# Differential attention on one core: the product with V moved behind the scores and into the turn's PSUM banks, fill split by kind of turn

## The chip, the core and the metric

The kernel runs on one core of one Trainium2 chip. The core has five engines that run side by side, each through its own list of instructions in order: TensorE (PE; its weight loads are shown apart as PEld), VectorE (DVE), ScalarE (ACT), GpSimd (POOL) and SyncE (SP, which here only issues transfers). They wait for each other by semaphores. The metric is the device time of one execution in microseconds (us); less is better.

## What is computed

One layer of an encoder with two branches, on a sequence of 1024 tokens of width 1024, in float32. The part that the change touches is the attention branch; the other branch (a state-space scan) and the projections around both are as before.

```
q = partial_rope(q); k = partial_rope(k)          # 4 heads, 2 halves of 64 each
def block(qblk):                                  # 128 queries
    sc = jnp.einsum('bqhcd,bkhcd->bhcqk', qblk, k) * scale
    p = jax.nn.softmax(sc, axis=-1)
    w = p[:, :, 0] - lam * p[:, :, 1]
    return jnp.einsum('bhqk,bkhe->bqhe', w, v)
o = rmsnorm(o, g_subln) * (1.0 - lam_init)
attn_branch = (o.reshape(b, s, ATTN_WIDTH) * jax.nn.silu(z_a)) @ w_up_attn
merged = jax.nn.sigmoid(g_a) * attn_branch + jax.nn.sigmoid(g_s) * ssm_branch
return x + gate[:, None, :] * (merged @ w_out)
```

Float32 products are made of three matmuls each, on operands that are cut into a high and a low part (`split`: ACT copies the high part, DVE or POOL subtracts it and leaves the low part).

## The kernel before

The program has five stretches: input norm and the first projections, the state-space branch, its gate and up-projection, the attention (stage 3, some 464 to 762 us of the trace), and the last two projections. The change lies in stage 3 and in the few us behind it.

**Turns.** Stage 3 goes through 32 turns g = 0 to 31, eight per head (head g // 8, and i = g % 8 within it), each for 128 queries, and two more (32, 33) that finish. PE's list for a turn, before the change: `qk(g)`, the scores, eight matmuls of 512 columns (`sc`, lines 1423 and 1424) into two tiles of two banks; fill; in every odd turn from 3 on `pv`, the product of two finished turns with V, 24 matmuls of 256 columns (`pv`, line 1465); `transpose_w(g-1)`, eight transposes of the weights `e` of the turn before (`tp<-cst,e`, line 1454); fill again. Meanwhile DVE takes the maximum of the scores (`nm`, line 1425, two reductions of 1024), ACT the exponentials (`e<-sc`, two), and DVE the mix of the two softmax halves of the turn before (`mix(g-1)`: `zr`, `wm`, and `e<-e,wm` of 1024 columns). The transposes of turn g wait for this mix. Behind them ACT copies the high part (`wth`, two of 512) and DVE makes the low part (`wtl`, two), which `pv` reads in one of the next two turns.

**Fill.** Between these stands work that needs nothing of the turn: the projections of q, k and v of the next head (heads 0 to 2) and gates (head 3). `drive` takes units of fill off the generator `s3_fill` whenever `s3_main` yields an amount: FA = 3.1 behind the scores and FB = 1.0 behind the transposes (2.45 and 1.0 from turn 24 on). One unit is three matmuls of 512 columns (`mm<-hh,wh`, `hl,wh`, `hh,wl`, line 217); a *block* below is one such unit. Eight blocks make half a projection, whose result ACT evicts (`rq`, `vt` or `side`). Small follow-up steps hang on the fill (`with_pend`, `rope_unit`): the rotation of q and k of the next head takes a shuffle on DVE into the tile `rs` (tag "tb", one buffer), three operations on POOL (times sine, times cosine, sum), and later ACT's copy `rh` and POOL's low part. The weights of the next projection are cut by ACT (`wh`) and POOL (`wl`).

**Per head.** `spot(s, g)` puts three things of a head into fixed turns of the next head, by the table `EV`: `make_v` (eight transposes of v, evicted by ACT `vh` and DVE `vl`) at the end of turn i = 1, `o_turn` (eight transposes of the finished output, evicted by ACT) at the end of i = 2, `o_norm` from the end of i = 3 on (eight short squares on ACT, `jk`; the rest in one go on DVE in i = 4; the scaling `o<-o,nry` on POOL), and `o_back` (eight transposes back, evicted by DVE `of`) at the end of i = 5, behind which SP stores the result.

**PSUM.** Eight banks: four for scores (tag "sc"), two of `ps_mm` (tag "mm") and two of `ps3` (tag "tp"). The pair "mm" is used by fill in turn with `pv`; the pair "tp" by the transposes of weights, V and output. A tile takes the older bank of its pair and waits until that was evicted. The order of every engine is the order in which the program records its instructions; no scheduler changes it.

Of the kernel before, what the change touches and what calls it, by code (L numbers as in the profile page):

```python
# [18 lines left out]
P = 128  # L19
# [47 lines left out]
def tile_hybrid_block(  # L67
# [1389 lines left out]
    def pv(p):  # L1457
# [3 lines left out]
        ps = ps_mm.tile([P, 512], F32, tag="mm", name="pv")  # L1461
# [19 lines left out]
    def o_norm(h, e=G, big=None):  # L1481
        H = heads[h]
        on, zr = H["on"], H["zr"]
        ss = po.tile([P, 8], F32, tag="oss", name="oss")
        if big is None:
            for t in range(8):
                jk = po.tile([P, P], F32, tag="jk", name="jk")
                act(jk, on[:, t], AF.Square, scale=zr[:, t, 0:1], accum_out=ss[:, t:t + 1])
            yield
        else:  # L1490
            z2 = po.tile([P, 8], F32, tag="jk", name="z2")
            for hf in range(2):
                act(big[:, hf * 512:hf * 512 + 512], H["o"][:, hf * 512:hf * 512 + 512], AF.Square)
            yield
            mul(z2, zr[:, :, 0], zr[:, :, 0])
            V.tensor_reduce(out=ss, in_=big[:].rearrange("p (t e) -> p t e", t=8), axis=AX.X, op=ALU.add)
            mul(ss, ss, z2)
        res = []
        for _ in rsqrt_gen(po, ss, 8, 1.0 / P, "o", res):
            yield  # L1500
        rs = res[0]
        mul(rs, rs, zr[:, :, 0])
        yield
        mul(on, on, bc(rs[:], 2, [P, 8, P]), e)
# [15 lines left out]
    def s3_main():  # L1520
# [6 lines left out]
        def spot(s, g):  # L1527
# [3 lines left out]
            if (i, s) == EV["v"] and h < 4:  # L1531
                make_v(h)
            if (i, s) == EV["turn"]:
                o_turn(h - 1)
            if (i, s) == EV["za"]:
                load_za(h - 1)
            if (i, s) == EV["sq"]:
                gens[h] = o_norm(h - 1)
                next(gens[h])
            if (i, s) == EV["norm"]:  # L1540
                run_all(gens[h])
            if (i, s) == EV["back"]:
                of = o_back(h - 1)
                SP.dma_start(out=ofd[h - 1], in_=of)

        for g in range(NG + 2):
            fa, fb = (FA, FB) if g < 24 else (LA, LB)
            if g < NG:
                qk(g)
            if 1 <= g <= NG:  # L1550
                mix(g - 1)
            spot(0, g)
            yield fa
            spot(1, g)
            if g >= 3 and g % 2 == 1:
                pv((g - 3) // 2)
            if 1 <= g <= NG:
                transpose_w(g - 1)
            spot(2, g)
            yield fb / 2  # L1560
            spot(3, g)
            yield fb / 2
# [225 lines left out]
```

## Time and profile before

| | before |
|---|---|
| median of 3 runs | 928.51 us (928.42 to 929.39) |
| the profiled execution: its time, its span | 930.2 us, 928.3 us |
| mean granted TensorE clock | 0.986 |
| busy: PE, PEld, DVE, ACT, POOL | 95%, 79%, 71%, 40%, 18% of the span |
| instructions | 12225 |
| last chain: PE, DVE, ACT, issue | 68%, 19%, 5%, 3% of the span |

The page and the answers give times from the start of the span. A row of the view of waits says which engine (and line) waited for whom, how long in total, how often, and the longest. A row of the timeline gives the start, the time from the first start to the last end, engine, line, operation, out<-in, sizes, how many were merged, and in brackets the idle time of the engine before it and what ended it. Matmuls overlap: one that takes 0.39 us is followed by the next 0.23 us later. A row of the view by lines ends with busy time, mean duration in ns, and the idle time before the group. A row of the view by windows gives the stretch, its length, busy time of the five engines, and the granted clock.

### The profile page before, as it was taken

What the parts mean: (1) busy time and instruction counts of PE and PEld (TensorE: products, weight loads), DVE (VectorE), ACT (ScalarE), POOL (GpSimd) and SP (SyncE); (2) the same over time, 40 slices, a digit from 0 to 9 for tenths busy, and PEclk for the clock granted to TensorE, in tenths of its full rate; (3) what the DMA queues carried; (4) which work ended last, traced back from release to release, by engine and by line L of the source; (5) the groups of instructions that cost most, each with busy time, mean ns of one, the idle gap of its engine ahead of it and who ended that gap; (6) DMA issues with size and microseconds to landing.
All of it is one profiled execution on the core that took longest, in us unless ns stands there. A gap on an engine that the chain in (4) does not pass through costs nothing.

```text
span 928.3 us, 12225 instructions
## 1 busy us (share of the span) xinstructions
PE 882.2 (95%) x4528; PEld 731.3 (79%) x4528; DVE 662.2 (71%) x1234; ACT 375.4 (40%) x652; POOL 164.9 (18%) x128
## 2 busy tenths in 40 slices
PE   5999999999999998999999999998998999999996
PEld 4878878888888886787778877787777788888885
DVE  5987999998999964673667576755866655573465
ACT  6753532322222253301365456545645544232222
POOL 1001000000000004222234425435411111340000
PEclk9899899999999999999999999999999999999998
DMA  9926223243433554593433313313123123958022
GB/s 297 301 74 182 87 74 116 82 125 96 129 99 91 168 167 175 185 351 122 113 81 91 80 34 103 97 51 85 61 71 89 49 89 116 339 183 304 13 88 95
DMA packets 106478, 119.57 MB, mean 129 GB/s; under 512 B 7587, under 2 KB 87696, under 8 KB 106418
## 3 DMA queue, kind: packets, MB, share of 16 engines
q1 hardware_dynamic: 104628, 114.08, 40.0%
q10 hardware_dynamic: 1614, 4.51, 1.2%
q8 instruction: 36, 0.59, 0.3%
q0 software_dynamic: 176, 0.20, 0.1%
q14 instruction: 24, 0.20, 0.1%
HBM read 78.46 MB, written 27.73 MB: 114 GB/s over the span
## 4 chain that ended last, share of the span: by engine, by line
PE 68%; DVE 19%; ACT 5%; issue 3%; DMA 2%; POOL 1%; SPq 1%; ACTq 0%; DVEq 0%
PE mm L217 38%; PE op L1707 10%; PE pv L1465 5%; DVE nm L1425 3%; PE tp L1454 3%; PE sc L1423 2%; PE sc L1424 2%; ACT e L99 2%; DVE acc L96 2%; DVE cb L78 2%; PE yp L1050 1%; DVE wl L78 1%; PE w L1002 1%; DVE e L96 1%; DVE wtl L78 1%
## 5 line engine op out<-in xcount | busy, mean ns | idle before, releaser
L217 PE MATMUL mm<-hh,wh 128*128 128x512 f32 x592 | 238.1, 402 | 0.5 <-ACT o L99 0.5
L217 PE MATMUL mm<-hh,wl 128*128 128x512 f32 x592 | 232.0, 392 | 0.0
L217 PE MATMUL mm<-hl,wh 128*128 128x512 f32 x592 | 231.8, 392 | 0.0
L217 PEld LDWEIGHTS mm<-hh,wl 128*128 128x128 f32 x592 | 111.7, 189 | 24.1 <-DVE wl L78 0.5
L217 PEld LDWEIGHTS mm<-hh,wh 128*128 128x128 f32 x592 | 111.9, 189 | 23.5 <-issue 1.6
L217 PEld LDWEIGHTS mm<-hl,wh 128*128 128x128 f32 x592 | 112.0, 189 | 20.9
L99 ACT ACTIVATE e<-sc,nm 128x1024 f32<-128x1024 f32 x64 | 71.1, 1114 | 71.8 <-DVE nm L1425 71.8
L78 DVE TENSOR_TENSOR wtl<-tp,wth 128x512 fp32r<-128x512 f32 x64 | 41.2, 686 | 70.7 <-ACT wth L99 70.7
L1425 DVE TENSOR_REDUCE nm<-sc 128x1 f32<-128x1024 f32 x64 | 75.4, 1219 | 22.4 <-PE sc L1424 21.6
L78 POOL TENSOR_TENSOR wl<-wr,wh 128x1024 fp32r<-128x1024 f32 x22 | 53.5, 2430 | 185.9 <-ACT wh L99 185.8
L99 ACT ACTIVATE wh<-wr 128x1024 fp32r<-128x1024 f32 x49 | 51.7, 1057 | 64.4 <-DMA pad<-pt 21.2
L99 ACT ACTIVATE side<-mm 128x512 f32<-128x512 f32 x48 | 28.6, 597 | 107.2 <-PE mm L217 78.9
L1423 PE MATMUL sc<-kk,qq 128*128 128x512 f32 x128 | 50.6, 395 | 1.6 <-issue 1.6
L1707 PE MATMUL op<-woh,ml 128*128 128x512 f32 (+1 forms) x136 | 51.7, 380 | 0.0
L1707 PE MATMUL op<-woh,mh 128*128 128x512 f32 (+1 forms) x136 | 51.6, 380 | 0.0
L1707 PE MATMUL op<-wol,mh 128*128 128x512 f32 (+1 forms) x136 | 51.6, 380 | 0.0
L1424 PE MATMUL sc<-kk,qb 128*128 128x512 f32 x128 | 50.1, 391 | 0.0
L96 DVE SCALAR_TENSOR_TENSOR e<-e,wm 128x1024 f32<-128x1024 f32 x32 | 45.3, 1416 | 1.1
L78 DVE TENSOR_TENSOR wl<-wr,wh 128x1024 fp32r<-128x1024 f32 x27 | 32.9, 1223 | 17.9 <-ACT wh L99 17.8
L1465 PE MATMUL pv<-wth,vh 128*128 128x256 f32 x128 | 37.5, 293 | 5.5 <-ACT rq L99 2.9
L1454 PE MATMUL tp<-cst,e 128*128 128x128 f32 x256 | 33.8, 276 | 6.7 <-DVE e L96 3.9
L942 POOL MEMSET rt<- 64x4 f32 x8 | 0.8, 98 | 217.6 <-ACT rt L99 217.6
(366 smaller groups left out, 1751.7 us busy)
## 6 DMA issues: line engine op xcount, KB each, us to landing
wr<-in_w_in_dram SPq DMA_DIRECT2D x40, 512.0 KB
wa<-in_w_ada_dram SPq DMA_DIRECT2D x16, 512.0 KB
x<-in_x_dram SPq DMA_DIRECT2D x8, 512.0 KB
gsd<-side SPq DMA_DIRECT2D x8, 512.0 KB
gad<-side SPq DMA_DIRECT2D x8, 512.0 KB
gt<-gsd SPq DMA_DIRECT2D x8, 512.0 KB
wg<-in_w_ada_dram SPq DMA_DIRECT2D x8, 512.0 KB
pad<-pt ACTq DMA_DIRECT2D x8, 512.0 KB
```

Source lines behind the costliest of these rows:

```text
L78: (e or V).tensor_tensor(out=o, in0=a, in1=b, op=op)
L96: V.scalar_tensor_tensor(out=o, in0=a, scalar=s, in1=b, op0=op0, op1=op1)
L99: A.activation(out=o, in_=i, func=f, **kw)
L217: PE.matmul(out=ps, lhsT=a[:, k, off:off + P], rhs=r[:, k, sl], start=(n == 0), stop=(n == 3 * K - 1))
L1002: PE.matmul(out=wp[q][:, c4, :], lhsT=gt[:, q, c4, :], rhs=ut[:, c4, :], start=True, stop=True)
L1050: PE.matmul(out=yp[:, c4, :], lhsT=cb[:, q, c4, :, :, 1].rearrange("p t h -> p (t h)"), rhs=z[:, q, c4, :], start=False, stop=(q == 1))
L1423: PE.matmul(out=sc[:, sl], lhsT=H["qq"][:, cc, tok], rhs=H["kk"][:, cc, sl], start=True, stop=False)
L1424: PE.matmul(out=sc[:, sl], lhsT=qb_t[g // 2][:, cc, tb], rhs=H["kk"][:, cc, sl], start=False, stop=True)
L1425: V.tensor_reduce(out=nm[:, cc:cc + 1], in_=sc, axis=AX.X, op=ALU.max, negate=True)
L1454: PE.transpose(ps[:, k, :], e[:, kt * P:kt * P + P], ident)
L1465: PE.matmul(out=ps[:, 0:256], lhsT=a[:, kt, :], rhs=r[:, kt, :], start=(n == 0), stop=(n == 23))
L1707: PE.matmul(out=ps[:, 0:n], lhsT=a[:, k, tok], rhs=r[:, k, lo:lo + n], start=(i == 0), stop=(i == 23))
```

## The change

`pv` takes its bank from the pair "tp" in place of "mm", and stands in odd turns right behind the scores, ahead of all fill. The fill behind the scores is one unit more in even turns and one less in odd ones (FD = 1.0), and each of the two amounts is yielded in halves, with a spot between. `make_v` moves to right behind the scores of turn i = 2, `o_turn` to the middle of the fill of the same turn, `o_back` to right behind the scores of i = 6. `o_norm` is cut into pieces, one per spot (three spots a turn): each half of the output is squared by ACT into a tile with the tag "tb" (512 columns) and summed by DVE; then three small DVE steps per spot. The form for head 3 (`s3_tail`) is cut alike. All amounts of work of PE stay the same.

```diff
--- before.py
+++ after.py
@@ -1458,7 +1458,7 @@
         h, q = divmod(p, 4)
         H = heads[h]
         wh, wl = wt_t.pop(p)
-        ps = ps_mm.tile([P, 512], F32, tag="mm", name="pv")
+        ps = ps3.tile([P, 512], F32, tag="tp", bufs=2, name="pv")
         n = 0
         for kt in range(8):
             for a, r in ((H["vh"], wh), (H["vh"], wl), (H["vl"], wh)):
@@ -1480,28 +1480,30 @@
 
     def o_norm(h, e=G, big=None):
         H = heads[h]
-        on, zr = H["on"], H["zr"]
+        on, zr, o = H["on"], H["zr"], H["o"]
         ss = po.tile([P, 8], F32, tag="oss", name="oss")
-        if big is None:
-            for t in range(8):
-                jk = po.tile([P, P], F32, tag="jk", name="jk")
-                act(jk, on[:, t], AF.Square, scale=zr[:, t, 0:1], accum_out=ss[:, t:t + 1])
-            yield
-        else:
-            z2 = po.tile([P, 8], F32, tag="jk", name="z2")
-            for hf in range(2):
-                act(big[:, hf * 512:hf * 512 + 512], H["o"][:, hf * 512:hf * 512 + 512], AF.Square)
-            yield
-            mul(z2, zr[:, :, 0], zr[:, :, 0])
-            V.tensor_reduce(out=ss, in_=big[:].rearrange("p (t e) -> p t e", t=8), axis=AX.X, op=ALU.add)
-            mul(ss, ss, z2)
+        z2 = po.tile([P, 8], F32, tag="z2", name="z2")
+        for hf in range(2):
+            sl = slice(hf * 512, hf * 512 + 512)
+            if big is None:
+                jk = p3.tile([P, 512], F32, tag="tb", name="sq")
+            else:
+                jk = big[:, sl]
+            act(jk, o[:, sl], AF.Square)
+            yield
+            V.tensor_reduce(out=ss[:, 4 * hf:4 * hf + 4], in_=jk.rearrange("p (t e) -> p t e", t=4) if big is not None
+                            else jk[:].rearrange("p (t e) -> p t e", t=4), axis=AX.X, op=ALU.add)
+        mul(z2, zr[:, :, 0], zr[:, :, 0])
+        mul(ss, ss, z2)
+        yield
         res = []
-        for _ in rsqrt_gen(po, ss, 8, 1.0 / P, "o", res):
-            yield
+        for n, _ in enumerate(rsqrt_gen(po, ss, 8, 1.0 / P, "o", res)):
+            if n % 3 == 2:
+                yield
         rs = res[0]
         mul(rs, rs, zr[:, :, 0])
-        yield
         mul(on, on, bc(rs[:], 2, [P, 8, P]), e)
+        yield
 
     def o_back(h):
         H = heads.pop(h)
@@ -1528,42 +1530,41 @@
             h, i = divmod(g, 8)
             if g < 8:
                 return
-            if (i, s) == EV["v"] and h < 4:
+            if (i, s) == (2, 0) and h < 4:
                 make_v(h)
-            if (i, s) == EV["turn"]:
+            if (i, s) == (2, 1) and h < 4:
                 o_turn(h - 1)
-            if (i, s) == EV["za"]:
+                gens[h] = o_norm(h - 1)
+            elif h in gens and next(gens[h], gens) is gens:
+                gens.pop(h)
+            if (i, s) == (5, 0):
                 load_za(h - 1)
-            if (i, s) == EV["sq"]:
-                gens[h] = o_norm(h - 1)
-                next(gens[h])
-            if (i, s) == EV["norm"]:
-                run_all(gens[h])
-            if (i, s) == EV["back"]:
-                of = o_back(h - 1)
-                SP.dma_start(out=ofd[h - 1], in_=of)
+            if (i, s) == (6, 0):
+                assert h not in gens
+                SP.dma_start(out=ofd[h - 1], in_=o_back(h - 1))
 
         for g in range(NG + 2):
             fa, fb = (FA, FB) if g < 24 else (LA, LB)
+            odd = g % 2
+            fa += FD * (1 - 2 * odd)
             if g < NG:
                 qk(g)
             if 1 <= g <= NG:
                 mix(g - 1)
+            if g >= 3 and odd:
+                pv((g - 3) // 2)
             spot(0, g)
-            yield fa
+            yield fa / 2
             spot(1, g)
-            if g >= 3 and g % 2 == 1:
-                pv((g - 3) // 2)
+            yield fa / 2
             if 1 <= g <= NG:
                 transpose_w(g - 1)
+            yield fb / 2
             spot(2, g)
             yield fb / 2
-            spot(3, g)
-            yield fb / 2
-
-    FA, FB = 3.1, 1.0
+
+    FA, FB, FD = 3.1, 1.0, 1.0
     LA, LB = 2.45, 1.0
-    EV = {"v": (1, 3), "turn": (2, 3), "sq": (3, 3), "norm": (4, 0), "za": (5, 0), "back": (5, 3)}
     fill3 = with_pend(s3_fill(), 2)
     drive(s3_main(), fill3)
     p3.release()
@@ -1589,6 +1590,7 @@
         for h in range(3):
             ofl.append(op.tile([P, S], F32, tag="sg", bufs=3, name="ofl"))
             SP.dma_start(out=ofl[h], in_=ofd[h])
+        next(norm)
         yield 3.0
         run_all(norm)
         for h in range(3):
```

How instructions move on three engines is shown by the order of their lists, since the diff doesn't tell. First PE in turn 10, from the transposes of the weights (`tp<-cst,e`) to the next scores before, where `tp<-cst,o` are those of the output and `mm` is fill:

```order
L1454 MATMUL tp<-cst,e 128x128 x8
L217 MATMUL mm<-hh,wh 128x512
L217 MATMUL mm<-hl,wh 128x512
L217 MATMUL mm<-hh,wl 128x512
L1478 MATMUL tp<-cst,o 128x128 x8
L217 MATMUL mm<-hh,wh 128x512
L217 MATMUL mm<-hl,wh 128x512
L217 MATMUL mm<-hh,wl 128x512
```

and now in the same turn, from the last score matmul on (`tp<-cst,vt` are the transposes of v):

```order
L1424 MATMUL sc<-kk,qb 128x512
L1391 MATMUL tp<-cst,vt 128x128 x8
L217 MATMUL mm<-hh,wh 128x512
L217 MATMUL mm<-hl,wh 128x512
L217 MATMUL mm<-hh,wl 128x512
L217 MATMUL mm<-hh,wh 128x512
L217 MATMUL mm<-hl,wh 128x512
L217 MATMUL mm<-hh,wl 128x512
L217 MATMUL mm<-hh,wh 128x512
L217 MATMUL mm<-hl,wh 128x512
L217 MATMUL mm<-hh,wl 128x512
L1478 MATMUL tp<-cst,o 128x128 x8
```

The transposes of v, which stood at the end of turn 9, and those of the output now stand three blocks apart in one turn; turns 18 and 26 are alike.

ACT in turns 18 and 19, before, from the exponentials of turn 18 (`e,zz`) on; `wh` belongs to the next projection's weights, `rq` and `rh` to the rotation:

```order
L99 ACTIVATE e,zz<-sc,nm 128x1024 x2
L99 ACTIVATE rq<-mm 128x512
L99 ACTIVATE wh<-wr 128x1024
L99 ACTIVATE wth<-tp 128x4x128 x2
L99 ACTIVATE o<-tp 128x512 x2
L99 ACTIVATE rh<-rq 128x512
L99 ACTIVATE e,zz<-sc,nm 128x1024 x2
L99 ACTIVATE rq<-mm 128x512
L99 ACTIVATE o<-pv 128x256
```

and now:

```order
L99 ACTIVATE e,zz<-sc,nm 128x1024 x2
L99 ACTIVATE vh<-tp 128x512 x2
L99 ACTIVATE rq<-mm 128x512
L99 ACTIVATE wh<-wr 128x1024
L99 ACTIVATE o<-tp 128x512 x2
L99 ACTIVATE rh<-rq 128x512
L99 ACTIVATE wth<-tp 128x4x128 x2
L99 ACTIVATE sq<-o 128x512
L99 ACTIVATE e,zz<-sc,nm 128x1024 x2
L99 ACTIVATE o<-pv 128x256
L99 ACTIVATE sq<-o 128x512
```

The copy `rh` stands ahead of the turn's two `wth` where it stood behind them, and two squares of half the output stand around the exponentials of turn 19.

DVE in turns 11 and 12, before, from the mix of turn 11 on (`rqv`, `nri`, `nry`, `nrt` are small steps of the output norm):

```order
L96 SCALAR_TENSOR_TENSOR e<-e,wm 128x1024
L78 TENSOR_TENSOR wtl<-tp,wth 128x4x128 x2
L1322 STREAM_SHUFFLE rs<-rq 128x512
L1425 TENSOR_REDUCE nm<-sc 128x1 x2
```

and now:

```order
L96 SCALAR_TENSOR_TENSOR e<-e,wm 128x1024
L1494 TENSOR_REDUCE oss<-sq 128x4 x2
L78 TENSOR_TENSOR z_4933<-zr 128x8
L78 TENSOR_TENSOR oss<-oss,z_4933 128x8
L78 TENSOR_TENSOR wtl<-tp,wth 128x4x128 x2
L93 TENSOR_SCALAR rqv<-oss 128x8
L91 TENSOR_SCALAR nri<-rqv 128x8
L93 TENSOR_SCALAR nry<-nri 128x8
L1322 STREAM_SHUFFLE rs<-rq 128x512
L1425 TENSOR_REDUCE nm<-sc 128x1 x2
```

Two reductions and five small steps stand between the mix of turn 11 and the maxima of turn 12 that had none there; before, all small steps stood behind the mix of turn 12.

## Rows read from the trace of the kernel before

**Rows 1.** Waits of PE alone, 464 to 770 us: who waited for whom, total, times, longest.

```profile
PE tp L1454 <- DVE e L96: 3.9, 6, 1.2
PE pv L1465 <- ACT rq L99: 2.9, 3, 1.9
PE tp L1454 <- DVE rqv L93: 2.6, 3, 1.5
PE tp L1513 <- DVE wtl L78: 2.0, 3, 1.1
PE pv L1465 <- ACT side L99: 1.9, 2, 1.3
PE tp L1391 <- DVE wtl L78: 1.7, 3, 1.0
...
PE tp L1478 <- DVE wtl L78: 1.1, 3, 0.4
PE pv L1465 <- ACT vt L99: 0.7, 2, 0.6
PE mm L217 <- ACT o L99: 0.5, 1, 0.5
```

**Rows 2.** Timeline of PE: transposes that did not wait (537.25), and that did (556.09).

```profile
536.98 0.39 PE L217 MATMUL mm<-hh,wl 128*128 128x512 f32 x1
537.25 0.41 PE L1454 MATMUL tp<-cst,e 128*128 128x128 f32 x2
...
554.91 0.39 PE L217 MATMUL mm<-hl,wh 128*128 128x512 f32 x1
555.14 0.39 PE L217 MATMUL mm<-hh,wl 128*128 128x512 f32 x1
556.09 1.06 PE L1454 MATMUL tp<-cst,e 128*128 128x128 f32 x8 [0.56 <-DVE e L96]
```

**Rows 3.** View by windows, 643.4 to 646.9 us: busy times, then the granted clock (0.51).

```profile
643.40:646.90 3.50, 3.50 (x19) 3.50 (x18) 0.00 (x0) 0.11 (x1) 3.42 (x3) 0.51 0.96 230
```

**Rows 4.** Timeline of POOL, ACT and PE, turns 18 and 19.

```profile
632.60 2.37 POOL L78 TENSOR_TENSOR wl<-wr,wh 128x1024 fp32r<-128x1024 f32 x1 [11.13 <-ACT wh L99]
...
637.55 1.28 POOL L78 TENSOR_TENSOR rq<-rq,rs 128x512 f32<-128x512 f32 x1
...
638.86 0.63 ACT L99 ACTIVATE rh<-rq 128x512 fp32r<-128x512 f32 x1 [3.13 <-POOL rq L78]
...
642.22 0.39 PE L1465 MATMUL pv<-wth,vh 128*128 128x256 f32 x1 [1.93 <-ACT rq L99]
```

**Rows 5.** Timeline of turn 10, which starts at 550.81 us with its first score matmul.

```profile
550.81 0.40 PE L1423 MATMUL sc<-kk,qq 128*128 128x512 f32 x1
...
551.94 2.36 DVE L1425 TENSOR_REDUCE nm<-sc 128x1 f32<-128x1024 f32 x2 [0.30 <-PE sc L1424]
...
554.33 1.12 ACT L99 ACTIVATE e<-sc,nm 128x1024 f32<-128x1024 f32 x1
...
554.65 1.29 DVE L96 SCALAR_TENSOR_TENSOR e<-e,wm 128x1024 f32<-128x1024 f32 x1
...
555.91 1.06 ACT L99 ACTIVATE wh<-wr 128x1024 fp32r<-128x1024 f32 x1
...
556.86 1.08 ACT L99 ACTIVATE wth<-tp 128x512 fp32r<-128x512 f32 x2
...
557.49 1.29 DVE L78 TENSOR_TENSOR wtl<-tp,wth 128x512 fp32r<-128x512 f32 x2 [0.59 <-ACT wth L99]
```

**Rows 6.** View by lines with shapes apart: a square of 512 columns, a small norm step.

```profile
L99 ACT ACTIVATE sq<-o 128x512 f32<-128x512 f32 x2 | 1.1, 624 | 0.0
...
L96 DVE SCALAR_TENSOR_TENSOR nrt<-nrt,rqv 128x8 f32<-128x8 f32 x12 | 2.0, 166 | 0.4
```

**Rows 7.** Timeline: a mix on DVE with POOL at work, and a POOL operation beside a mix.

```profile
574.60 2.39 DVE L96 SCALAR_TENSOR_TENSOR e<-e,wm 128x1024 f32<-128x1024 f32 x1
...
639.57 2.26 POOL L78 TENSOR_TENSOR rq<-rq,rh 128x512 fp32r<-128x512 f32 x1 [0.74 <-ACT rh L99]
```

More of the change, by code (lines that the diff above doesn't have):

```diff
@@ L1482, in o_norm @@
         H = heads[h]
-        on, zr = H["on"], H["zr"]
+        on, zr, o = H["on"], H["zr"], H["o"]
         ss = po.tile([P, 8], F32, tag="oss", name="oss")
-        if big is None:
-            for t in range(8):
-                jk = po.tile([P, P], F32, tag="jk", name="jk")
-                act(jk, on[:, t], AF.Square, scale=zr[:, t, 0:1], accum_out=ss[:, t:t + 1])
-            yield
-        else:
-            z2 = po.tile([P, 8], F32, tag="jk", name="z2")
-            for hf in range(2):
-                act(big[:, hf * 512:hf * 512 + 512], H["o"][:, hf * 512:hf * 512 + 512], AF.Square)
-            yield
-            mul(z2, zr[:, :, 0], zr[:, :, 0])
-            V.tensor_reduce(out=ss, in_=big[:].rearrange("p (t e) -> p t e", t=8), axis=AX.X, op=ALU.add)
-            mul(ss, ss, z2)
+        z2 = po.tile([P, 8], F32, tag="z2", name="z2")
[6 more added lines that the diff above has]
+            act(jk, o[:, sl], AF.Square)
+            yield
+            V.tensor_reduce(out=ss[:, 4 * hf:4 * hf + 4], in_=jk.rearrange("p (t e) -> p t e", t=4) if big is not None
[3 more added lines that the diff above has]
+        yield
         res = []
-        for _ in rsqrt_gen(po, ss, 8, 1.0 / P, "o", res):
-            yield
+        for n, _ in enumerate(rsqrt_gen(po, ss, 8, 1.0 / P, "o", res)):
+            if n % 3 == 2:
+                yield
         rs = res[0]
         mul(rs, rs, zr[:, :, 0])
+        mul(on, on, bc(rs[:], 2, [P, 8, P]), e)
         yield
-        mul(on, on, bc(rs[:], 2, [P, 8, P]), e)
     def o_back(h):
```

## The prediction

> **What bounds the kernel now.** I read the waits of PE first, since PE is busy nearly throughout and the change leaves its work alone: a gain can only be idle time of PE. In stage 3 [rows 1] PE waits 26 times, 17.3 us in all, for three reasons. The transposes of the weights wait for the mix (3.9 and 2.6 us; the name `rqv` in one row stands where the mix itself came last). The product with V waits for an eviction of fill by ACT (2.9, 1.9 and 0.7), because it shares the pair "mm" with fill. The transposes of v and the output wait for `wtl` (2.0, 1.7, 1.1), because they follow the weights' transposes through the pair "tp". The last row is fill that waits for the product's eviction (0.5).
>
> The idle time understates a wait. Transposes that did not wait start 0.27 us behind the last fill matmul; those that waited started 0.95 us behind it, with 0.56 shown as idle [rows 2]. So 0.12 us comes on top of each: 26 x 0.12 = 3.1, and 20.4 us is what PE loses. One wait, 1.93 us in turn 19 [rows 4], was followed by a stretch at the lower of the two clock levels, 1.2 GHz: 3.5 us at a granted 0.51 [rows 3], which is 1.7 us of work lost. **Together 22.1 us can be had.**
>
> A clean turn, in us from its first score matmul [rows 5]: both maxima are done at 3.5, the mix runs from 3.84 to 5.13, the weights' transposes can start at 5.28 [rows 2]. The second exponential ends at 4.64. Counted from the start of the weights' transposes, `wth` runs from 0.8 to 1.85 and `wtl` from 1.4 to 2.7. A fill or score matmul takes 0.227 (554.91 to 555.14 in [rows 2]), so a block takes 0.68, the scores 1.82, the 24 half-wide products with V 2.72. Eight transposes hold PE for about 0.8 (1.06 less the overlap).
>
> **What the change removes.** All of [rows 1] goes from its place.
> - With "mm" left to fill alone, a half projection has the 5.4 us of the other half's eight blocks for its eviction: the 5.5 us of `pv` waits and the 0.5 end.
> - `pv` right behind the scores needs `wtl` of the turn before. It is due 0.8 + 0.68 + 1.82 = 3.3 us after those transposes began; the first `wtl`, which also frees its bank, is done at 2.1, and the second, needed for the second half, at 2.7. The eight scores cover it, if ACT is in time.
> - In turn, the weights' second half takes the bank of `pv`, evicted by ACT behind the second exponential at about 5.1; it is due after 6.5. The two to four blocks between cover that.
> - The weights' transposes of an even turn are due at 1.82 + 6 x 0.68 = 5.9, of an odd one at 1.82 + 2.72 + 3 x 0.68 = 6.6; ready at 5.3 in a clean turn. The one unit more of fill does this: 6.5 us go.
> - The transposes moved off the turn's end no longer meet `wtl`: 4.8 us.
>
> **What it adds**, with the place of each:
> - *v and output in one turn (10, 18, 26).* `vh` stands behind the second exponential on ACT: 4.64 to 5.24 and to 5.8, at the length of a `wth`. `vl` follows behind the mix, 5.27 to 5.95 and to 6.6, at the length of a `wtl`. The output's transposes are due at 1.82 + 0.86 + 2.04 = 4.75, but take the banks of v: first half at 6.0, second at 6.65 in place of 5.2. That is 1.45 us, three times: **4.4**. Behind PE in that wait stand three blocks and the weights' transposes, so the turn grows by it.
> - *Turn 1* has no `pv` yet and loses one unit: its wait grows from 0.6 to **1.3**.
> - *The chain on POOL.* In [rows 4] `wl` and the three rotation steps take 6.2 us (632.60 to 638.83), and ACT idled 3.13 us for `rh`. In turn 10 the two `vh` delay `wh`, so this chain runs from 7.2 to 13.4, while the turn lasts 10.7. The square `sq` shares the tag "tb" with `rs`, so it holds ACT until 2.8 us into turn 11. There nothing of PE is late, but the norm's sums (two at half of 1.18, rounded to 0.65), five small steps (0.17 each [rows 6]) and the shuffle reach DVE ahead of the maxima of turn 12, which start at 2.5 in place of 1.13. With a mix that meets POOL at work (2.39 in place of 1.29 us [rows 7]) the transposes are ready at 7.5, due at 5.9: **1.6**; turn 13 in the same way **0.5**.
> - *Turn 18* is worse: here `rh` stands ahead of `wth` on ACT. It waits for the chain until 13.5, the turn ends at 11.4, so `wth` comes at 14.2 and the first `wtl` is done at 15.5. `pv` of turn 19 is due at 13.2: **2.35**, and since that idle time is longer than the 1.93 that was followed by the lower clock, I count **1.7** for a stretch of the same kind. The maxima of turn 19 come late too, but the wait of `pv` covers this. Turns 20 and 21, with small steps and shuffle ahead of their maxima: **1.0** and **0.6**.
> - *Last head* (no rotation): small steps ahead of the maxima of turns 28 and 29, and `of` in 30: **0.75**.
> - *Turn 33*: one block between the weights' transposes and `pv`, due after 1.5, bank free at 2.1: **0.6**.
>
> I cost at nothing: ACT's eight short squares per head against two of 0.62 us [rows 6] (ACT has gaps; uncovered it would be a gain); the transposes back at the start of turn 14, 22 and 30, whose `of` follows the mix at 5.1 to 6.7 and whose banks are due at 7.5 (at 6.1 in turn 30, counted); POOL's scaling, done a turn ahead of them; SP's store of `of`, which now waits in its queue until the next turn's 6.7 us with loads of k behind it that turn 16 or 24 needs, a turn later; the head-3 norm, whose steps only start earlier under the 19 blocks of fill that cover it.
>
> **Sum.** 4.4 + 1.3 + 2.1 + 4.05 + 1.6 + 0.75 + 0.6 = 14.8 us of new waits against 22.1: **7.3 us less**. The profiled execution, 930.2 us (span 928.3), would take 922.9; it lies 1.7 us above the median of 928.5, so the forecast for the median is **921.2 us**.
>
> The only price that is not in the trace is the half-size reduction; between 0.6 (half) and 1.18 (no gain from size) it moves turns 12, 20 and 28 by up to 0.5 each. The mix beside POOL lies between 1.29 and 2.39; I took the upper for turns 12, 13 and 21, and with the lower 3 us go. The clock may or may not fall in turn 19: 1.7 either way, and once more in turn 12.
>
> The Trainium skill ("SBUF — State Buffer", section "Who interferes with whom") says of the port that VectorE and GpSimd share that whoever issues first holds it for its whole instruction and the other blocks. The trace agrees in part: in [rows 7] the mix loses 1.1 us beside a POOL step at one place, and POOL's step lasts 2.26 in place of 1.28 beside a mix at the other. By this rule a late mix loses only the rest of the POOL step under way, so the sum's 3 us for three turns could be anything from nothing to 3.9.
>
> **Rivals.**
> 1. *ACT is not held up.* If POOL's chain is early enough, the turns 11 to 13 and 19 to 21 keep only their small steps, some 3 us in place of 7.75: 10.1 us of new waits, **916.5 us**. For it: ACT's list is shorter by six instructions per head. Against it: the 3.13 us of [rows 4] is there today, with nothing ahead of the chain that the change takes away. Chance 0.17.
> 2. *The pair "tp" becomes the bound.* Three kinds of tile, and now `pv`, go through two banks. With ACT 1.6 us late, as behind a `wh` and an `rq`, the bank would come free at 3.7 where `pv` needs it at 3.3: 0.4 in each of some eight odd turns with one block, 3 us, and **924.2 us**. The 2.1 against 3.3 speaks against it in clean turns. The Trainium skill ("Perfetto Trace Analysis", section "Matmuls") asks that independent groups rotate through different banks so that an eviction overlaps the next group; by that rule the move into the crowded pair costs, while fill has two banks that it doesn't need. Chance 0.10.
> 3. *Slower: ACT, in order, stands behind POOL at many places.* Besides the `rh` of turn 18, the `sq` of turns 10 and 18 and the `rh` of turns 12 and 20 wait for the same chain with `wth` or exponentials queued behind them. If five such places each cost what turn 19 costs today (2.05 of wait and 1.7 of clock, [rows 3, 4]), the new waits are 4.4 + 1.3 + 0.75 + 0.6 + 18.8 = 25.9, 3.8 more than what goes: **932.3 us**. It decides from four such places on. Against it: in turns 11 and 13 PE has a product and three blocks before it needs `wth`. Chance 0.07.
> 4. *It only shifts the waits*, with about 22 us of new ones, as several small delays of the maxima pass from turn to turn: **928.5 us**. Chance 0.08. That the change doesn't do what it says can be excluded: PE's order shows each move.
>
> **Numbers.** The forecast has 0.58, its own range 917.5 to 924. The range of 913.5 to 926.5 takes in rivals 1 and 2 and the bounds of the unsure prices. A measurement of this kernel can tell some 0.2% (1.9 us) from no change. Faster by more: forecast, rivals 1 and 2, 0.85; same: rival 4, 0.08; slower: 0.07.
>
> **What would show it.** Right: the waits of PE list no `pv` for `rq`, `side` or `vt`; about 1.5 us for the output's transposes on `vl` in turns 10, 18 and 26; a wait of over 2 us of `pv` in turn 19 with ACT's `rh` on POOL ahead of it; transposes waiting for the mix in turns 1, 12, 20. Wrong: `pv` waiting for `wtl` in most odd turns (rival 2), a granted clock that falls at several places (rival 3), or the total of PE's waits in stage 3 outside 8 to 16 us of shown idle time.

## The result, and the profile after

| | before | after |
|---|---|---|
| median | 928.46 us (927.33 to 929.39, 4 runs) | 919.29 us (915.63 to 920.49, 4 runs) |
| ratio | | 0.9892, 95% interval 0.9869 to 0.9916 |
| profiled execution: time, span | 930.2 us, 928.3 us | 915.63 us, 913.8 us |
| stage 3, from its first score matmul to the first matmul on `oh` | 323.29 us | 311.90 us |

The kernel is 9.2 us faster; 921.2 us was forecast, with 7.3 us less than before. The profiled execution of after is the fastest of its four, so its span shows more than the median does (14.5 us). Two rows of PE's timeline for each kernel bound stage 3. Before:

```profile
464.20 0.47 PE L1423 MATMUL sc<-kk,qq 128*128 128x512 f32 x1 [0.42 <-issue]
...
787.49 0.39 PE L217 MATMUL mm<-oh,wh 128*128 128x512 f32 x1
```

After:

```profile
460.99 0.48 PE L1423 MATMUL sc<-kk,qq 128*128 128x512 f32 x1 [0.65 <-issue]
...
772.89 0.40 PE L217 MATMUL mm<-oh,wh 128*128 128x512 f32 x1
```

The stage is 11.4 us shorter. (Counted to the first matmul on `oh`, it takes in the fill behind turn 31, so it ends at 787 us in before and not at 762.) What follows it takes 140.8 us before and 140.9 after. The remaining 3.2 us lie ahead of it, where the change edits nothing. There before has a stretch at half the clock (from 356.7 us, 3.4 us long, so 1.7 us lost) which this execution of after has not; the other 1.5 us are not explained. Which single stretches fall to half the clock is not the same in these two executions, so I compare experiments below by the stage's length and by PE's waits, and use the medians as a second witness.

The waits of PE in after, 461 to 774 us, answer to [rows 1] (line, whom it waited for, total us, times, longest):

```profile
PE tp L1478 <- DVE vl L78: 3.1, 3, 1.0
PE pv L1465 <- DVE wtl L78: 2.7, 3, 2.0
PE tp L1454 <- DVE nry L78: 2.6, 2, 1.8
PE tp L1454 <- DVE nrt L78: 2.1, 2, 1.2
PE sc L1423 <- issue: 1.9, 2, 1.2
PE tp L1454 <- DVE e L96: 1.1, 1, 1.1
```

Without the row of the stage's start (`issue`), 11.6 us in 11 waits stand against 17.3 in 26. Every row of [rows 1] with `pv` behind an eviction of fill is gone, and so are the waits of the transposes of v and output for `wtl`. New are the output behind `vl` and `pv` behind `wtl`. Measured from the start of one PE instruction to the next, beyond the distance without a wait, the waits are 13.25 us against 21.4, so 8.2 of the 11.4 us are these waits. Another 1.7 is the clock, which stayed up. About 1.6 lies between the transposes of one group, in steps too short for the view of waits.

Turn 19 of after answers to [rows 4]. POOL, ACT and PE, from the timeline:

```profile
631.72 1.29 POOL L78 TENSOR_TENSOR rq<-rq,rs 128x512 f32<-128x512 f32 x1
...
633.05 0.63 ACT L99 ACTIVATE rh<-rq 128x512 fp32r<-128x512 f32 x1 [5.39 <-POOL rq L78]
633.59 1.06 ACT L99 ACTIVATE wth<-tp 128x512 fp32r<-128x512 f32 x2
...
634.94 0.38 PE L1465 MATMUL pv<-wth,vh 128*128 128x256 f32 x1 [1.99 <-DVE wtl L78]
```

This is the chain that the prediction drew: ACT idles for `rh` (5.39 us, 3.13 before), `wth` is queued behind it, and `pv` waits. The view by windows right behind it shows a granted clock of 1.00, where before had 0.51 after a wait of 1.93 us [rows 3, 4]:

```profile
635.40:638.90 3.50, 3.50 (x28) 3.32 (x27) 3.43 (x6) 2.25 (x5) 0.00 (x0) 1.00 0.98 219
```

The largest miss is turn 13. DVE's timeline, turns 12 and 13 (the reading follows below):

```profile
569.22 2.40 DVE L96 SCALAR_TENSOR_TENSOR e<-e,wm 128x1024 f32<-128x1024 f32 x1
571.54 0.15 DVE L78 TENSOR_TENSOR nrt<-nry 128x8 f32<-128x8 f32 x1
571.73 2.25 DVE L96 SCALAR_TENSOR_TENSOR nrt<-nrt,rqv 128x8 f32<-128x8 f32 x1
574.01 1.22 DVE L96 SCALAR_TENSOR_TENSOR nry<-nrt,nry 128x8 f32<-128x8 f32 x1
575.26 0.17 DVE L78 TENSOR_TENSOR nrt<-nry 128x8 f32<-128x8 f32 x1
...
575.75 1.28 DVE L78 TENSOR_TENSOR wtl<-tp,wth 128x512 fp32r<-128x512 f32 x2
...
578.06 2.34 DVE L1425 TENSOR_REDUCE nm<-sc 128x1 f32<-128x1024 f32 x2
...
580.86 2.39 DVE L96 SCALAR_TENSOR_TENSOR e<-e,wm 128x1024 f32<-128x1024 f32 x1
```

POOL in the same stretch:

```profile
569.25 1.29 POOL L78 TENSOR_TENSOR rq<-rq,rs 128x512 f32<-128x512 f32 x1
571.53 2.42 POOL L78 TENSOR_TENSOR wl<-wr,wh 128x1024 fp32r<-128x1024 f32 x1 [0.99 <-ACT wh L99]
573.90 1.30 POOL L78 TENSOR_TENSOR rq<-rq,rh 128x512 fp32r<-128x512 f32 x1
```

And the waits of PE that come of it:

```profile
571.76 1.06 PE L1454 MATMUL tp<-cst,e 128*128 128x128 f32 x8 [1.22 <-DVE nrt L78]
...
576.49 0.38 PE L1465 MATMUL pv<-wth,vh 128*128 128x256 f32 x1 [0.44 <-DVE wtl L78]
...
583.39 0.85 PE L1454 MATMUL tp<-cst,e 128*128 128x128 f32 x6 [1.83 <-DVE nry L78]
```

A step on 128x8 elements that takes 0.17 us elsewhere [rows 6] lasted 2.25 us: it started 0.20 us behind POOL's `wl` and ended with it. The next lasted 1.22, to the end of POOL's `rq`. The step before them, which started within 0.01 us of `wl`, took 0.15. Some 3.1 us of DVE went there. `wtl` and both maxima stand behind these steps; the maxima of turn 13 began at 578.06, and the mix, beside POOL again, ended at 583.25, when PE had waited 1.83 us. (The names `nrt` and `nry` in PE's rows stand for the mix that came last, as `rqv` did in [rows 1].) The view of the tile `nrt` shows that it is not the step's own length (count, then min, median, max in ns):

```profile
L96 DVE SCALAR_TENSOR_TENSOR nrt<-nrt,rqv x12: 166/168/2246, 571.7 to 762.2; 128x8 f32<-128x8 f32 x12
```

### The profile page after: what moved, and what is told of

Its sections match the earlier page's. It is cut to its first block, busy times and chain, and to the rows that moved or that the text cites. A ratio compares the mean times of both kernels' runs of the same rounds, so it can differ in the third digit from the quotient of the medians.

```text
span 913.8 us, 12194 instructions
## 1 busy us (share of the span) xinstructions
PE 874.9 (96%) x4528; PEld 729.8 (80%) x4528; DVE 672.3 (74%) x1247; ACT 366.5 (40%) x610; POOL 164.2 (18%) x128
## 4 chain that ended last, share of the span: by engine, by line
PE 74%; DVE 17%; ACT 3%; issue 2%; DMA 2%; POOL 1%; SPq 0%; ACTq 0%; DVEq 0%
PE mm L217 44%; PE op L1709 10%; PE pv L1465 4%; PE tp L1454 3%; PE sc L1423 3%; PE sc L1424 3%; DVE acc L96 2%; DVE nm L1425 2%; PE yp L1050 1%; PE w L1002 1%; DVE cb L78 1%; DVE wl L78 1%; DVE e L96 1%; ACT e L99 1%; PE tp L963 1%
## 5 line engine op out<-in xcount | busy, mean ns | idle before, releaser
L217 PEld LDWEIGHTS mm<-hh,wh 128*128 128x128 f32 x592 | 111.8, 189 | 22.1 <-issue 1.7
L217 PEld LDWEIGHTS mm<-hl,wh 128*128 128x128 f32 x592 | 112.0, 189 | 20.4
L99 ACT ACTIVATE wth<-tp 128x512 fp32r<-128x512 f32 x64 | 34.8, 596 | 39.9 <-PE tp L1454 39.9
```

The costliest lines, as they stand in the source:

```text
L99: A.activation(out=o, in_=i, func=f, **kw)
L217: PE.matmul(out=ps, lhsT=a[:, k, off:off + P], rhs=r[:, k, sl], start=(n == 0), stop=(n == 3 * K - 1))
```

## The experiments

All are edits of the changed kernel unless said otherwise. "Stage" is the length as in the table above. Three theories were open: that the gain comes from the product's bank (the pair "tp" in place of "mm"), from its place behind the scores, or from the finer parts (fill by kind of turn, V and output between fill, small steps).

### Bank, fill and place, one at a time

**pv_in_mm**, the product back in the bank pair of fill, at its new place:

```
-        ps = ps3.tile([P, 512], F32, tag="tp", bufs=2, name="pv")
+        ps = ps_mm.tile([P, 512], F32, tag="mm", name="pv")
```

> The changed kernel, with the product with V back in the pair of banks that fill uses, but still right behind the scores. Theory (the shared pair was the cause of the waits for fill's evictions): banks are taken in turn, so after each product the next half projection takes the bank of the half that has just ended and must wait for ACT's eviction, at least 0.8 us (0.6 and its start), and more where exponentials stand ahead. With some 10 to 15 such places I expect 10 to 20 us more than the changed kernel's 919.3 us, 929 to 939, and waits of PE's fill for ACT in the list. Rival (the place behind the scores was what helped): within 2 us of 919.3, no such waits.

Measured: 921.38 us (916.49 to 923.81, 5 runs), ratio 0.9908, interval 0.9874 to 0.9941; stage 316.5 us, with two stretches at half the clock in it, some 313.0 without. PE's waits show one of fill behind the product's eviction, in turn 19:

```profile
PE mm L217 <- ACT o L99: 1.4, 1, 1.4
```

The theory of the bank, and with it my figure, fell: behind the scores the pair "mm" does as well within some 1 us of stage length (313.0 against 311.9), and the intervals of the two ratios overlap.

**no_fill_split**: every turn has the same fill. (The amounts that `drive` takes are not blocks: a block of three matmuls takes 0.66 of an amount, so FD = 1.0 is a block and a half. Up to turn 23, the six or seven blocks that a turn had before became seven or eight in even turns and four or five in odd ones.)

```
-    FA, FB, FD = 3.1, 1.0, 1.0
+    FA, FB, FD = 3.1, 1.0, 0.0
```

> The changed kernel with equal fill in odd and even turns (FD = 0). Theory: without the product, even turns now have five blocks behind the scores where they had four or five before the change, so the weights' transposes are due at 5.2 us and ready at 5.3: 0.1 us in a clean even turn, 0.7 more in turns 12 and 20, 1.4 less in turn 13, 0.7 less in turn 1. 0 to 2 us more than 919.3 us. Rival (the prediction's words: the one unit more of fill takes away the 6.5 us of waits for the mix): 5 us or more above, 924 to 927, with waits for the mix in most even turns.

Measured: 919.74 us (918.70 to 920.19, 4 runs), 0.9899 (0.9868 to 0.9930); stage 312.2 us, waits 13.3, both as in after. The rows of the transposes behind the mix:

```profile
PE tp L1454 <- DVE nrt L78: 3.8, 3, 1.9
PE tp L1454 <- DVE e L96: 3.0, 3, 1.4
```

With one of 0.2 (behind `nry`) that is 7.0 us, against 6.5 in [rows 1] and 5.8 in after. By turns, the split takes away the waits of turns 6, 24, 28 and 30 (4.3 us together) and brings those of turns 13 and 19 (4.7 us), which this kernel has not; the rest is smaller and goes both ways. The split trades one set of waits for another and is worth nothing that these runs can tell. Turn 19 shows why its wait comes and goes: with equal fill, `rh` of turn 18 stands behind the turn's two `wth` in ACT's list (`wth` at 631.30 us, `rh` at 636.24), so the product does not wait for POOL's chain; in after it stands ahead of them.

**pv_only**: the kernel before with the product moved and given the bank "tp", and nothing else.

```
-        ps = ps_mm.tile([P, 512], F32, tag="mm", name="pv")
+        ps = ps3.tile([P, 512], F32, tag="tp", bufs=2, name="pv")
...
+            if g >= 3 and g % 2 == 1:
+                pv((g - 3) // 2)
             spot(0, g)
             yield fa
             spot(1, g)
-            if g >= 3 and g % 2 == 1:
-                pv((g - 3) // 2)
```

> The kernel before with one edit: the product with V right behind the scores, in a bank "tp". If the place does it: stage 313 to 316 us against 323.3, some 920 to 922 us; the waits left are those at V and output (6 us) and at the late weights (turn 19). If the parts of the change only work together: 319 us or more, 925 us or more.

Measured: 919.49 us (919.07 to 920.31, 4 runs), 0.9910 (0.9895 to 0.9925); stage 314.5 us. Nearly the whole gain is there already: its median is within 0.2 us of that of after, and the intervals of the ratios overlap. Its waits of PE:

```profile
PE tp L1454 <- DVE e L96: 4.9, 7, 1.4
PE tp L1454 <- DVE rqv L93: 2.7, 3, 1.5
PE tp L1513 <- DVE wtl L78: 2.0, 3, 1.1
PE tp L1391 <- DVE wtl L78: 1.7, 3, 1.0
```

Against [rows 1] only the `pv` rows (and the fill behind them) are gone; the waits for the mix (7.6 us against 6.5) and for `wtl` are still there.

**pv_back**: the reverse, all of the change but the product, which is at its old place and in "mm".

```
-        ps = ps3.tile([P, 512], F32, tag="tp", bufs=2, name="pv")
+        ps = ps_mm.tile([P, 512], F32, tag="mm", name="pv")
...
-            if g >= 3 and odd:
-                pv((g - 3) // 2)
             spot(0, g)
             yield fa / 2
             spot(1, g)
             yield fa / 2
+            if g >= 3 and odd:
+                pv((g - 3) // 2)
```

> The changed kernel with the product with V at its old place (ahead of the transposes of the mix, behind the turn's fill) and in its old bank "mm"; the split fill and the new places of V, output and norm steps stay. If the place of the product is what the change gains by, most of the 11.4 us of the third stage come back: stage 319 to 323 us, some 926 us, with waits of the transposes on the mix and of the fill on the product's eviction as in rows 1. If the new places of V and output and the smaller fill pieces make the gain, it stays at 312 to 314 us and 919 to 921.

Measured: 935.41 us (933.27 to 936.08, 4 runs), 1.0076 (1.0058 to 1.0094), so slower than before; stage 329.2 us. Both of my numbers were missed, in the direction that makes the place weigh more; 8.5 us of the stage are the clock, and without them it is 320.6. Two rows of its waits, and the product of turn 19 in PE's timeline:

```profile
PE pv L1465 <- ACT rq L99: 8.8, 2, 6.1
PE pv L1465 <- ACT side L99: 3.5, 1, 3.5
```

```profile
651.78 0.58 PE L1465 MATMUL pv<-wth,vh 128*128 128x256 f32 x1 [6.14 <-ACT rq L99]
```

Behind the fill the product meets a bank that was filled just before and that ACT must evict, and ACT has `rh`, which waits 5.37 us for POOL, `wth`, the exponentials and two `sq` in front. Four stretches of this stage are at the lower level of the clock, three of them at the end of a wait of 2.5 to 3.5 us or up to 1.2 us behind it; the fourth begins inside this wait:

```profile
649.10:655.90 6.80, 4.12 (x19) 4.13 (x20) 3.08 (x7) 1.59 (x4) 2.84 (x3) 0.50 0.79 227
```

So it is the place that decides: pv_back and pv_in_mm differ in it alone, and with the pair "mm" at the old place the product waits 14.0 us for the evictions of fill, at the new one not at all (its 2.3 us there are for `wth` and `wtl`). The stages differ by 12.7 us, or 7.6 without the stretches at half the clock. The old place with the pair "tp" was not tried. Without the move the finer parts cost 7 us against before, by the profiles all of it clock (without the stretches at half the clock, the stage is 320.6 us against 321.6). With the move they gain 2.6 us in the profile and nothing that the medians can tell (919.49 against 919.29).

### What the waits left are made of

**wl_on_dve**: the weights' low part in stage 3 on DVE, to relieve POOL.

```
     FA, FB, FD = 3.1, 1.0, 1.0
+    w_state["eng"] = V
```

> The changed kernel with the low part of fill's weights (wl, 2.4 us each on POOL) made by DVE (1.2 us) in stage 3. Theory (POOL's chain behind wl holds ACT's rh and with it wth and the product of turn 19; and an operation of POOL under way holds up DVE's small norm steps in turns 12 and 13): turn 19's wait of 2.2 us goes, turn 13's of 2.6 falls to under 1, turn 20 and 21 fall by half. 3 to 6 us less, 913 to 916, and no row of the product waiting for wtl above 0.5 us. Rival (DVE is the engine behind these waits): ten times 1.2 us more on DVE delay the maxima, and the time rises by 2 to 5 us.

Measured: 917.46 us (916.20 to 919.01, 4 runs), 0.9874 (0.9845 to 0.9903); stage 311.7 us, waits 13.1. Turn 13's wait of the product goes and that of the transposes falls only from 1.96 to 1.7; turn 19's falls only from 2.15 to 1.71, and turns 20 and 21 keep theirs. The edit does not take `wl` out of turn 18's chain, though. DVE makes it ahead of the shuffle that starts the rotation, so the shuffle now stands behind `wl`, which waits for `wh`:

```profile
629.74 1.23 DVE L78 TENSOR_TENSOR wl<-wr,wh 128x1024 fp32r<-128x1024 f32 x1 [0.63 <-ACT wh L99]
...
630.89 0.73 DVE L1322 STREAM_SHUFFLE rs<-rq 128x512 f32<-128x512 f32 x1
...
635.63 0.63 ACT L99 ACTIVATE rh<-rq 128x512 fp32r<-128x512 f32 x1 [4.95 <-POOL rq L78]
```

In after the shuffle was done before `wl` began. So ACT's idle time for `rh` falls only from 5.39 to 4.95 us, and the run does not show what the chain would cost without `wl`.

**o_turn_later**: the output's transposes one turn behind V's (`sq` goes into the tile `of`, since the other has no room then).

```
-            if (i, s) == (2, 1) and h < 4:
+            if (i, s) == (3, 1) and h < 4:
-            if (i, s) == (5, 0):
+            if (i, s) == (6, 0):
                 load_za(h - 1)
-            if (i, s) == (6, 0):
+            if (i, s) == (7, 0):
```

> The changed kernel with the output's transposes one turn later (i = 3, and what follows a turn later), the squares written into the tile that later takes silu(z). Theory (the wait of the output's transposes comes from taking v's two banks in the same turn): the three rows of 1.0 us idle (1.17 each in starts) are gone, 3.5 us; but turn 18 is then shorter while POOL's chain is not, so the product of turn 19 waits about 1.2 longer, and the small steps move to turns 12 to 13 and 20 to 21 with similar waits. 1 to 3 us less than 919.3. Rival (any eight transposes in that place cost this): the wait shows up in the new place and the time stays within 1 us.

Measured: 919.57 us (917.85 to 921.97, 4 runs), 0.9897 (0.9866 to 0.9928); stage 312.6 us, with two stretches at half the clock, some 309.2 without. The three waits behind `vl` (3.5 us from the starts) are gone, but the turn that is now shorter makes the product of turn 19 wait longer:

```profile
PE pv L1466 <- DVE wtl L78: 4.9, 3, 4.3
```

A wait that stands in front of a late result only hides a part of it.

**steps_pool**: the norm's 128x8 steps on POOL, but for the two with integers; the step of the iteration with three operands is written as two there.

```
-            mul(t, y, y)
+            mul(t, y, y, e)
...
+                mul(t, t, v, e)
+                ts(t, t, -0.5, 1.5, ALU.mult, ALU.add, e)
+                mul(y, y, t, e)
...
-        mul(ss, ss, z2)
+        mul(ss, ss, z2, e)
```

> [...] If the small steps on DVE wait for the POOL operation under way and hold up the low part and the maxima behind them, the waits in turn 13 fall from 2.6 us to 0.8 or less and those in turns 20 and 21 from 2.0 to 0.6 or less: stage 308.5 to 309.5 us, some 916. If those waits come from ACT or from the late weights, the stage stays at 311 to 313 us and the waits where they are; if POOL becomes late by its own small steps, turn 19's wait of 2.15 us grows.

Measured: 918.53 us (916.01 to 920.07, 4 runs), 0.9896 (0.9875 to 0.9917); stage 312.7 us with one stretch at half the clock. Turn 13's 2.6 us are gone altogether, but turn 20 waits 2.8. DVE's timeline there:

```profile
647.40 0.17 DVE L91 TENSOR_SCALAR nri<-rqv 128x8 int32<-128x8 int32 x1 [3.15 <-POOL rqv L93]
```

The integer step was placed right behind the POOL step that it reads; POOL came to that only behind the rotation, and DVE with both maxima behind it stood still for 3.15 us.

**steps_apart**: the same, with one place of the program between the two.

```
-            if n % 3 == 2:
+            if n in (0, 2, 5, 8, 11):
                 yield
```

> As steps_pool (the norm's small steps on POOL), but with the two integer steps, which stay on DVE, one place later than the step on POOL that they read. If DVE's halt in turn 20 of steps_pool (3.1 us of DVE idle at the first integer step, then 2.8 us of PE's wait for the mix) came from waiting in order for POOL, turn 20's wait falls to 1 us or less and turns 12 and 13 stay free of theirs but for the mix's own 1.2: stage 308.5 to 310 us, some 914 to 916 us. If the wait in turn 20 has another cause (the late weights of turn 19), it stays at 2 us or more.

Measured: 916.12 us (915.75 to 916.94, 4 runs), 0.9870 (0.9852 to 0.9887); stage 309.6 us. The waits:

```profile
PE tp L1485 <- DVE vl L78: 3.1, 3, 1.0
PE pv L1472 <- DVE wtl L78: 2.2, 2, 2.0
PE tp L1522 <- POOL o L78: 1.9, 2, 1.3
```

Turns 20 and 21 are free of the mix, turns 12 and 13 keep 0.9 and 0.6. New is the output's way back, which waits for POOL's scaling (1.9 us), as POOL now comes to it later. Both theories of the small steps are shown by this pair: they cost by their place on DVE beside POOL, and by waiting in order for POOL.

### A version that beats both

**comb_wl**: output later, steps on POOL, weights' low part on DVE, and one more edit that was to take `rh` out of `wth`'s way:

```
-            pend.extend([turn, skip, skip, cut])
+            pend.extend([turn, skip, skip, skip, cut])
```

> Four edits on the changed kernel at once: the output's transposes one turn later, the weights' low part on DVE, the norm's small steps on POOL, and the cut into high and low of the rotated q and k one piece of fill later. If the waits left in the changed kernel (13.2 us by the starts of PE's work) have these four causes, 3 to 6 us of them stay: stage 302 to 305 us, some 909 to 913 us. If the waits only move (as turn 19's did when the output alone was moved): 8 us or more of waits, stage 307 us or more, 914 us or more.

Measured: 933.04 us (931.48 to 935.37, 5 runs), 1.0058 (1.0040 to 1.0076); stage 327.5 us. The waits name the edit that failed:

```profile
PE sc L1431 <- DMA kk<-rq: 9.8, 4, 4.9
```

`kk` is loaded from `rh` and `rq` once both are cut; one piece of fill later the loads come too late for the first scores of turns 8 and 16, and three stretches at half the clock (8.5 us lost) lie around the first scores of turns 8, 16 and 24. Waits for the mix of 6.2 us in six places stay as well.

**o_later_steps** (o_turn_later with steps_apart, and turn 1 without its smaller fill) and **o_later_steps_wl** (with the low part on DVE too). The amount of turn 1 rises from 2.1 to 4.1, which is three blocks (eight in place of five), so the "one piece more of fill in turn 1" of the text on o_later_turn1 is three blocks. The second one differs from comb_wl by more than the later cut: also by steps_apart and by turn 1.

```
-            fa += FD * (1 - 2 * odd)
+            fa += FD * (1 - 2 * odd) if g > 1 else FD
```

> steps_apart with the output's transposes one turn later as well, and no smaller piece of fill in turn 1. If the waits add up: turn 1's 1.25 us, the 3.5 us of the output behind V and the 2.6 us of turn 13 go, turn 19's grows from 2.2 to 4.4 as in o_turn_later: stage 306 to 308 us, some 912 to 915 us. If waits only move, 311 us or more.

> o_later_steps with the weights' low part on DVE: comb_wl without the later cut of q and k. If comb_wl lost by its transfers of k (13 us of waits in front of the scores of turns 8, 16 and 24, and the clock after them), those waits are gone: stage 305 to 308 us, some 911 to 914 us, and turn 19's wait below 2 us. If DVE with the weights' low part is itself too late, turns 8, 16 and 24 wait again and it is above 920.

Measured: **909.98 us** (908.10 to 911.62, 4 runs), 0.9800 (0.9783 to 0.9817), stage 304.9 us; and 910.38 us (908.64 to 912.13, 4 runs), 0.9805 (0.9788 to 0.9822), stage 304.1 us. Both are some 9 us below the changed kernel; which of the two is faster the medians cannot tell. The largest waits of PE in o_later_steps:

```profile
PE tp L1462 <- DVE e L96: 1.5, 1, 1.5
PE mm L217 <- DVE of L96: 1.2, 1, 1.2
PE tp L1462 <- DVE vl L78: 0.7, 1, 0.7
PE pv L1473 <- DVE wtl L78: 0.3, 1, 0.3
```

Turn 19's wait is gone in both, where 4.4 us had been expected for the first. Neither has a wait of the scores for `kk`. The steps on POOL and the edit of turn 1 were then tried apart.

**o_later_turn1**: o_turn_later with only the edit of turn 1.

> o_later_steps with the norm's small steps back on DVE: the output's transposes one turn later and no smaller piece of fill in turn 1, nothing else. o_later_steps was 7 us below o_turn_later by the stage's length without its stretches at the lower clock (303.2 against 309.2), of which I had put 2.5 to the steps and 1.3 to turn 1; turn 19's wait of 4.4 us went as well, since one piece more of fill in turn 1 lets all later projections and their rotations end a piece earlier. If the piece does most of it: turn 19's wait is gone here too, 2 to 3 us of waits for small steps are back, stage 306 to 308 us, some 912 to 914 us. If the steps on POOL did it: turn 19's wait is back at 4 us and the stage at 309 us or more.

Measured: 912.01 us (911.10 to 913.19, 5 runs), 0.9821 (0.9792 to 0.9850); stage 305.6 us.

```profile
PE pv L1466 <- DVE wtl L78: 1.8, 2, 1.5
PE tp L1455 <- DVE nrt L78: 1.7, 3, 0.7
```

Turn 19's wait is gone here too (the 1.5 us of `pv` are now in turn 21), so the three blocks did it. With them, the projections of q and k and all that hangs on them (`wh`, POOL's chain, `rh`) come three blocks earlier in the turns, and the last stretch of fill behind turn 31 has three fewer: in o_later_steps the sum of the rotation ends at 622.5 us, ahead of turn 19's first score matmul at 626.4, where in after it ends at 633.0, behind that at 631.0. Without the stretches at half the clock the stage goes from 309.2 to 305.6 by the three blocks in turn 1 (1.3 of it is turn 1's own wait), and from there to 303.2 by the steps on POOL.

## Why the prediction was right, and where it was not

**What goes.** The waits of `pv` for fill, of fill for `pv` and of v and output for `wtl` went, as forecast. 22.1 us were put down for what goes; measured are 24.7: 21.4 of waits in place of 20.4 (a wait costs 0.15 to 0.16 beyond its idle time, not 0.12, counted against the 0.23 at which transposes that do not wait start in after, not the 0.27 of [rows 2]), 1.7 of clock, and 1.6 between transposes that the sum did not have. But two reasons were not borne out. "With 'mm' left to fill alone" is not what ended the `pv` waits: in pv_in_mm the pair is shared and they are gone all the same. And "the one unit more of fill does this: 6.5 us go" is right for the turns that it names and empty as a gain: no_fill_split has no such unit and the same length, since what the unit frees it costs mainly in turns 13 and 19.

**What is added.** 14.8 us were summed, 13.3 measured. By terms, as counted from starts:

| place | predicted | measured |
|---|---|---|
| output behind V, turns 10, 18, 26 | 1.45 each | 1.16, 1.17, 1.17 |
| turn 1 | 1.3 | 1.25 |
| turn 12 | 1.6 | 1.35 |
| turn 13 | 0.5 | 2.56 (0.60 of the product, 1.96 of the transposes) |
| turn 19, wait of the product | 2.35 | 2.15 |
| turn 19, clock | 1.7 | 0 |
| turns 20, 21 | 1.0, 0.6 | 1.05, 0.94 |
| last head, 28 to 30 | 0.75 | 0 |
| turn 33 | 0.6 | 0.45 |

The sum of what is added was right to 1.5 us by luck in part: 4.0 us of terms were too high (the clock 1.7, the output 0.85, the last head 0.75) and 2.5 too low. With 24.7 less 13.3 the stage gained 11.4 us where 7.3 was forecast; the median, 9.2 lower, lies closer to the forecast than the profiled stage does. The 24 products with V were priced at 2.72 us, by half of a 512-column matmul's 0.227; in after they start 0.118 us apart, 2.83 in all, which moves no term by more than 0.1. *Turn 13* was mis-sized by 2.1 us: the prediction priced it "in the same way" as turn 12, with small steps of 0.17, but of the nine steps ahead of its maxima two took 2.25 and 1.22. steps_pool, where these steps are off DVE, has no wait in turn 13. *The clock* of turn 19 was taken from one wait of nearly the same length; after the 1.99 us of this execution it did not fall. before had 0.51 after 1.93 us, pv_in_mm has a stretch at the lower level 1 us behind another wait of 1.93 us (turn 13), and o_turn_later, with 4.3, has one from 638.0 us on. So the length of one wait does not decide it by itself; what else does, these rows do not show.

**The port.** The prediction weighed the rule of the Trainium skill ("SBUF — State Buffer", section "Who interferes with whom") that of VectorE and GpSimd whoever issues first holds the shared port for its whole instruction. (The page calls the lock exclusive and says who holds it of VectorE's two-port modes; of an instruction with two inputs in SBUF, like the mix and the steps here, it says that it contends.) The trace agrees for the small steps: the 2.25 us of a 128x8 step are the rest of POOL's `wl`. For the mixes it agrees only in part: those at 569.22 and 580.86 us lost 1.1 us each to a POOL step that started 0.02 to 0.03 us behind them, so at that distance the order of the starts in the trace does not tell who is held up. I applied the rule to the long operations and not to the short ones, where the ratio is largest.

**Rivals.** Rival 1 (ACT not held up) is out by the 5.39 us of `rh`. Rival 2 (the pair "tp" the bound) asked for `pv` behind `wtl` in most odd turns; there are three such waits, 2.0 us of the 2.7 in turn 19, and pv_in_mm, which takes `pv` out of that pair, is 1 us longer and not shorter. Rival 3 (slower by ACT behind POOL in many places) did not come in after, but its mechanism is what pv_back shows: long waits of the product, the clock after them, and a time above before's. Rival 4 is out by the interval.

## What to carry to other kernels

In this kernel a consumer that needs a PSUM bank fared best at a place where the last user of that bank had long been evicted; moving it there (here: behind the scores) was worth the gain, and giving it another bank at most 1 us. Small steps on VectorE are not cheap by their size: they cost what is left of the GpSimd operation under way, and they cost it ahead of whatever is queued behind them, so put them on GpSimd itself, and put a step that reads such a result a good way behind it. Where filler work drives a chain of later steps, try some blocks more or fewer at the very start before tuning places in the middle: here three blocks took 3.6 us off o_turn_later (on the changed kernel alone they were not tried).

## What was not expected of the hardware

A VectorE operation on 128x8 elements, 0.17 us by itself, lasted 2.25 us beside a GpSimd operation of 2.42 us that started 0.20 us ahead of it. A shift on 128x8 integers, with one input, took 1.22 us in turn 20 of after beside a GpSimd operation of 1.31 us that started 0.11 us ahead of it. A 128x8 step on GpSimd takes 0.20 us (the three-operand one, written as two, 0.20 to 0.21 each); some sixteen of them per head made the scaling behind them late (1.9 us of PE's waits in steps_apart). VectorE's reductions from PSUM were not stretched in this way: the two maxima of turn 13, with GpSimd at work from 578.25 to 580.81 us, took 2.34 us together, against 2.36 in [rows 5].
